# The down-projection of a hybrid trunk: sums that go on in PSUM across groups of products, with operands kept in place

## The chip, the core and the metric

One core of one Trainium2 chip runs a two-layer hybrid encoder trunk in one launch. Five engines work side by side: TensorE (PE, with its weight loads as PEld), VectorE (DVE), ScalarE (ACT), GpSimd (POOL) and SyncE (SP), which here issues nearly all DMAs. Each takes its own instructions in order and waits on semaphores of the others. The metric is the time of one execution on the device, in microseconds.

## The reference

Each of DEPTH = 2 layers mixes tokens with three kinds of heads and then runs a gated feed-forward part. What the change touches is the last line, with D_FF = 2816, 1024 tokens and a width of 1024, all in float32:

```
hf = rms_norm(x, ffn_norm[l]) @ w_up[l]
gate, val = hf[..., :D_FF], hf[..., D_FF:]
gate = depthwise_conv(gate, conv_w[l], conv_b[l])
x = x + (gelu(gate) * val) @ w_down[l]
```

## The kernel before

Features lie on the partitions, 128 at a time, so the residual `X` is eight tiles of 128 x 1024. A layer runs the projections and the heads, the output projection (`out_proj`), then `up` and `down`.

`up` walks over 22 blocks `f` of 128 hidden features. For each, 84 matmuls of 128x512 make seven products (L1114); DVE adds them into `v` and `g` (L1121), `gate` scales and convolves (POOL L1154, L1155 and L1159; DVE L1156 and L1157; ACT L1158), DVE multiplies (L1144), and SP stores the block `t` to a scratch array in DRAM, `hid` in the profile's names (L1145). The next block's weights come as `wraw`; their split forms `wo` lie in the ring of ten `w` slots.

`down` computes a 1024 x 2816 by 2816 x 1024 product as a 2 x 2 block product with seven instead of eight multiplications: `W[k]` and `W[k + 11]` are the two halves of the hidden features, `h0` and `h1` the halves of outputs or tokens. Every operand is split in two, a rounded value and its rest (`split`, `split2`: ACT copies, DVE subtracts), and a product of two operands is three matmuls: high by high, high by rest, rest by high. A product thus takes 11 steps `k`, four column blocks `c` and three terms: 132 matmuls, 924 for seven, all at L1306. They run in four **groups**: groups 0 to 2 make two products each (`acc[0]` in the two `pa` tiles of two banks each, `acc[1]` in the four `pt` and `pb` banks), group 3 makes one. A group's steps run in the order that `orders` gives; the last three steps of a group are issued together, column by column (`DOWN_TAIL`), and `evacuate` empties each bank once, at its group's end.

The operands of a step come from `prep(g, k)`: up to five DMA loads of 256 KB (`load`, L1188, on SP), DVE differences and sums (`tt`, L1174), then the splits. Group 0 makes `dp` and `dq` (weights in half 0, hidden rows in half 1) and `dr = dp - dq`; the `k`-th pair lies in a ring that `DOWN_RINGS` names: `r` (8 slots), `w` (10) or `u` (13). Group 1 loads over `dp`, uses it up, and leaves `ds` for each `k`; group 2 loads `dz` and `dt`, adds `dz` to `ds`, and loads one half of `ds` anew for group 3. `dz`, `dy` and all the splits (`bo`, `bw`) share the 16 `x` slots, and `dt` has three half slots. The seven products go in part to several blocks of the output: groups 0 and 1 are copied to `du` tiles by ACT (L1256), and `late_adds` combines these on DVE during group 2, three operations a step, and adds them to `X`; groups 2 and 3 are added to `X` straight out of PSUM. The eight tiles `X` are loaded from DRAM (`mid`) in group 1, from step `DOWN_X` on.

The order on each engine isn't that of the code: a scheduler of the framework places each instruction when it can run by its own model, with the slots of the rings as limits, and the engines then keep that order.

Of the kernel before, what the change touches and what calls it, by code (L numbers as in the profile page):

```python
# [13 lines left out]
ALU = mybir.AluOpType  # L14
AX = mybir.AxisListType.X

P = 128
# [54 lines left out]
DOWN_RINGS = "rwrwrwwwuuu"  # L72
DOWN_ORDER = [10, 9, 8, 0, 2, 4, 1, 3, 5, 6, 7]
DOWN_X = 5
# [19 lines left out]
class Trunk:  # L94
# [1069 lines left out]

    def down(self, l, H, spill, out):
# [4 lines left out]
        X, kept, S, U, V, E, F, adds = [], {}, {}, [], [], [], [], []  # L1170
        orders = [list(range(n)), DOWN_ORDER, DOWN_ORDER[::-1], DOWN_ORDER[::-1]]

        def tt(out, a, b, op=ALU.subtract):
            nc.vector.tensor_tensor(out, a, b, op=op)  # L1174

        def split(src):
            o = self.split_x(src, None, self.xslot)
            return o[:, 0], o[:, 1]
# [11 lines left out]
        def prep(g, k):  # L1190
            if g == 0:
                slot = {"r": self.rslot, "w": self.wslot, "u": self.slot}[DOWN_RINGS[k]]

                p, q = kept[k] = slot([P, 2, 512], name="dp"), slot([P, 2, 512], name="dq")
                b = self.half([P, 512], "dt")
                load(p[:, 0], W[k][:, h0])
                load(b, H[k][:, h0])
                load(q[:, 0], W[k][:, h1])
                load(q[:, 1], H[k][:, h1])
                load(p[:, 1], H[k + n][:, h1])  # L1200
                one = split(p[:, 0]), split(b)
                r = self.slot([P, 2, 512], name="dr")
                tt(r, p, q)
                return [one, split2(r)]
            if g == 1:
                p, q = kept.pop(k)

                y = self.xslot([P, 2, 512], name="dy")
                load(p[:, 1], H[k][:, h0])
                load(y[:, 0], W[k + n][:, h1])  # L1210
                load(y[:, 1], H[k + n][:, h1])
                s = S[k] = (self.slot if len(S) < 9 else self.wslot)([P, 2, 512], name="ds")
                tt(p[:, 1], q[:, 1], p[:, 1])
                tt(y[:, 0], y[:, 0], q[:, 0], ALU.add)
                one = split(y[:, 0]), split(p[:, 1])

                tt(s, p, y)
                return [one, split2(s)]
            s = S[k]
            if g == 2:  # L1220

                z, b = self.xslot([P, 2, 512], name="dz"), self.half([P, 512], "dt")
                load(z[:, 0], W[k + n][:, h0])
                load(z[:, 1], H[k + n][:, h0])
                load(b, H[k + n][:, h1])

                tt(s, z, s, ALU.add)
                one = split(s[:, 0]), split(b)
                load(s[:, 0], W[k + n][:, h1])
                return [one, split2(z)]  # L1230
            return [None, split2(s)]

        def late_adds():

            for c2 in range(2):
                u, v, e, f = U[c2], V[c2], E[c2], F[c2]
                yield f, u, f
                for j in range(2):
                    x = X[2 * c2 + j][:, h0]
                    yield x, x, u[:, j]  # L1240

                yield v, v, f
                yield f, f, e
                yield e, e, v
                for j in range(2):
                    x, y = X[2 * c2 + j], X[4 + 2 * c2 + j]
                    yield x[:, h1], x[:, h1], f[:, j]
                    yield y[:, h0], y[:, h0], v[:, j]
                    yield y[:, h1], y[:, h1], e[:, j]
# [23 lines left out]
        for i, (g, k) in enumerate(steps):  # L1273
# [3 lines left out]
            if g == 2:  # L1277
                if m == 0:
                    adds = late_adds()
# [201 lines left out]
```

## Time and profile before

| | before |
|---|---|
| median of 3 runs | 2920.05 us (2918.1 to 2930.07) |
| the profiled execution | 2923.2 us |
| its span | 2921.4 us, 40354 instructions |
| mean granted TensorE clock | 0.987 |
| PE at L1306, layer 1 | from 1226.97 to 1468.40 us |
| PE at L1306, layer 2 | from 2675.20 to the last matmuls, which start at 2916.90 |

The profile follows one execution. Its rows name engine, line, operation, `out<-in` and shapes; what stands in brackets behind a row of the timeline is how long the engine sat idle before it, and what it then had waited for. A table of windows gives the busy time of each engine in stretches of the span, with the count of instructions, the TensorE clock that was granted (PEclk, 1.00 is full), the mean busy share of the 16 DMA engines and what they moved. The lines of the two tables above that carry the argument are quoted where they are used.

### The profile page before, as it was taken

The numbers are of one execution on the slowest core, as the hardware profiler recorded it, in microseconds if no ns is written. First come the engines' busy times: TensorE is split into PE (matmuls) and PEld (weight loads), VectorE is DVE, ScalarE is ACT, GpSimd is POOL, SyncE is SP. The second block draws the span as 40 slices with busy tenths as digits, with TensorE's granted clock in tenths as the row PEclk, the third lists the DMA queues.
The fourth block names the chain that finished last, engine by engine and source line by source line (L and its number), as shares of the span: only waits on it lengthen the run. The fifth ranks groups of instructions, "written<-read, shape, count | busy, mean of one in ns | idle before, by whom it ended". The sixth has DMA issues, their size and how long they took to land.

```text
span 2921.4 us, 40354 instructions
## 1 busy us (share of the span) xinstructions
PE 2797.9 (96%) x14984; PEld 2345.9 (80%) x14984; DVE 2260.8 (77%) x3082; ACT 1359.5 (47%) x2371; POOL 1236.8 (42%) x811
## 2 busy tenths in 40 slices
PE   8999999999999999899899999999999999998998
PEld 7999986777777787687699999777777787776876
DVE  5849678897788888888648495888967888888874
ACT  5526467786422222243435264677854222223432
POOL 2516545532366666410115265454323666664100
PEclk9999999999999999999999999999999999999999
DMA  4213262101222222654313043421022122226432
GB/s 146 84 32 102 73 155 69 44 16 65 94 73 86 73 87 80 216 181 154 103 53 84 24 113 99 113 69 44 15 88 85 66 87 80 84 76 248 166 124 96
DMA packets 152900, 273.64 MB, mean 94 GB/s; under 512 B 16512, under 2 KB 74112, under 8 KB 152704
## 3 DMA queue, kind: packets, MB, share of 16 engines
q1 hardware_dynamic: 142912, 241.71, 25.6%
q0 software_dynamic: 9792, 29.36, 3.8%
q8 instruction: 118, 1.93, 0.3%
q14 instruction: 78, 0.64, 0.1%
HBM read 201.80 MB, written 69.21 MB: 93 GB/s over the span
## 4 chain that ended last, share of the span: by engine, by line
PE 27%; DVE 9%; POOL 6%; DMA 5%; issue 3%; ACT 3%; SPq 0%; ACTq 0%; DVEq 0%; POOLq 0%
PE pa L269 5%; PE pa L281 4%; POOL ws L1059 3%; DVE wo L1064 3%; PE pb L860 2%; PE pa L774 2%; DMA wraw<-w_u 2%; PE pt L1306 2%; PE pa L1306 2%; PE pb L1306 2%; DMA dz<-hid 2%; PE pt L845 2%; POOL t L1159 1%; ACT wo L1063 1%; PE pb L619 1%
## 5 line engine op out<-in xcount | busy, mean ns | idle before, releaser
L1114 PE MATMUL pt<-bo,wo 128*128 128x512 f32 x1584 | 388.6, 397 | 29.6 <-DVE pu L1121 24.1
L1114 PEld LDWEIGHTS pt<-bo,wo 128*128 128x128 f32 x1584 | 297.0, 190 | 111.6 <-issue 35.1
L1114 PE MATMUL pb<-bo,wo 128*128 128x512 f32 x1584 | 381.7, 389 | 0.6 <-ACT rbc L1037 0.6
L1114 PEld LDWEIGHTS pb<-bo,wo 128*128 128x128 f32 x1584 | 297.0, 188 | 62.8 <-ACT rbc L1037 1.1
L281 PE MATMUL pa<-wh,xh 128*128 128x256 f32 (+1 forms) x864 | 263.6, 305 | 7.6 <-ACT xh L233 7.6
L281 PE MATMUL pa<-wh,xl 128*128 128x256 f32 (+1 forms) x864 | 262.1, 305 | 5.5 <-DVE xl L234 5.5
L774 PE MATMUL pa<-qk,qk 96*128 96x512 f32 (+1 forms) x896 | 258.1, 415 | 9.3 <-DMA qk<-bq 3.9
L281 PE MATMUL pa<-wl,xh 128*128 128x256 f32 (+1 forms) x864 | 262.0, 303 | 1.4 <-DVE wl L336 1.4
L1306 PE MATMUL pa<-bo,bo 128*128 128x512 f32 x792 | 206.9, 407 | 26.0 <-ACT bo L1016 22.1
L1064 DVE TENSOR_TENSOR wo<-ws,wo 128x512 fp32r<-128x512 f32 x176 | 216.0, 1244 | 8.6 <-ACT wo L1063 4.5
L1063 ACT ACTIVATE wo<-ws 128x512 fp32r<-128x512 f32 x176 | 102.0, 624 | 253.6 <-POOL ws L1059 209.9
L1306 PEld LDWEIGHTS pa<-bo,bo 128*128 128x128 f32 x792 | 152.3, 196 | 69.8 <-ACT bo L1016 28.6
L855 DVE TENSOR_TENSOR ptl<-pt,pth 128x512 fp32r<-128x512 f32 x240 | 161.9, 683 | 45.4 <-ACT pth L849 44.2
L774 PEld LDWEIGHTS pa<-qk,qk 96*128 96x128 f32 (+1 forms) x896 | 157.4, 191 | 40.0 <-issue 8.1
L809 DVE CUSTOM_DVE_ANT_0 pb<-pa,toep 128x1024 f32<-128x1024 f32 x128 | 153.7, 1218 | 45.1 <-PE pa L774 41.0
L849 ACT ACTIVATE pth<-pt 128x512 fp32r<-128x512 f32 x256 | 148.9, 597 | 76.3 <-PE pt L845 72.2
L793 POOL TENSOR_SCALAR pa<-pa,z 128x1024 f32<-128x1024 f32 x96 | 110.1, 1147 | 153.1 <-PE pt L845 102.8
L281 PEld LDWEIGHTS pa<-wh,xh 128*128 128x128 f32 x864 | 166.4, 193 | 7.7 <-ACT xh L233 7.6
L281 PEld LDWEIGHTS pa<-wh,xl 128*128 128x128 f32 x864 | 165.2, 192 | 6.1 <-DVE xl L234 5.9
L281 PEld LDWEIGHTS pa<-wl,xh 128*128 128x128 f32 x864 | 166.3, 192 | 1.9 <-DVE wl L336 1.6
L1064 DVE TENSOR_TENSOR wo<-wraw,wo 128x512 fp32r<-128x512 f32 x132 | 149.7, 1137 | 18.3 <-ACT wo L1063 16.1
L812 ACT ACTIVATE pb<-pb,nmb 128x1024 f32<-128x1024 f32 x128 | 147.1, 1151 | 32.7 <-DVE nmb L809 27.0
(324 smaller groups left out, 6900.0 us busy)
## 6 DMA issues: line engine op xcount, KB each, us to landing
wraw<-w_u SPq DMA_DIRECT2D x88, 512.0 KB, 4.0
hid<-t SPq DMA_DIRECT2D x44, 512.0 KB, 2.9
bk<-st SPq DMA_DIRECT2D x256, 48.0 KB, 1.7
qk<-bk POOLq DMA_DIRECT2D x32, 384.0 KB, 6.2
dt<-hid SPq DMA_DIRECT2D x44, 256.0 KB, 3.9
dp<-hid SPq DMA_DIRECT2D x44, 256.0 KB, 5.4
X<-xT SPq DMA_DIRECT2D x16, 512.0 KB, 5.3
wraw<-w_o SPq DMA_DIRECT2D x16, 512.0 KB, 3.7
```

Of the source, the lines that this page charges most:

```text
L269: nc.tensor.matmul(ps[:, hf * 512 : hf * 512 + 512], w, x[:, hf * 512 : hf * 512 + 512], start=first, stop=last)
L281: self.nc.tensor.matmul(ps, x[:, ts], w[:, k % kp, :cols], start=first, stop=last)
L774: nc.tensor.matmul(ps[:, hs], q[:rows, o + t * P : o + (t + 1) * P], kk[w][:rows, hs], start=w == 0, stop=w == 1)
L793: nc.gpsimd.tensor_scalar(e, e, z, 1.0, op0=ALU.mult, op1=ALU.mult)
L809: nc.vector.tensor_tensor_reduce(e, ps, self.toep[:, o : o + T], scale=-slope, scalar=3.0e38, op0=ALU.add, op1=ALU.min, accum_out=nm)
L812: nc.scalar.activation(e, e, AF.Exp, bias=nm, scale=-1.0, accum_out=z[:, t, i : i + 1])
L849: nc.scalar.activation(hi[:, kk], ps, AF.Copy)
L855: nc.vector.tensor_tensor(lo[:, kk], ps, hi[:, kk], op=ALU.subtract)
L1063: nc.scalar.activation(o[:, 0], src, AF.Copy)
L1064: nc.vector.tensor_tensor(o[:, 1], src, o[:, 0], op=ALU.subtract)
L1114: nc.tensor.matmul(ps, st, mv, start=k + u + v == 0, stop=k == 3 and u == 1)
L1306: nc.tensor.matmul(acc[j][c], a[u][:, c * P : (c + 1) * P], b[v], start=q + u + v == 0, stop=q == n - 1 and u == 1)
```

## The change

The seven products are grouped anew, so that one that goes to several output blocks is summed in one bank with the others that go there:

- Group 0 makes its two products in `acc[0]` and `acc[1]`. At its end DVE adds `acc[0]` to half `h0` of `X[c]`, and `acc[1]` to half `h1` of `X[4 + c]`; PSUM keeps both.
- Group 1 sums on into the same eight banks. At its end DVE adds both to half `h1` of `X[c]`.
- Group 2 sums on in `acc[0]` and starts `acc[1]` anew; at the end `acc[0]` goes to both halves of `X[4 + c]` (one 1024-wide addition from a broadcast bank), `acc[1]` to half `h0` of `X[c]`.
- Group 3 starts `acc[1]` anew and adds it to half `h0` of `X[4 + c]`.

So `du`, ACT's copies into it and `late_adds` are gone. `dp` and `dq` stay in their slots, loaded and computed over in place, through all four groups: steps 0 to 4 in `w` slots, steps 5 to 10 in `u` slots. Half loads go to `da` (half slots) in groups 0 and 1; group 2 has a further pair `dw`, in two `x` slots and then in `u` slots. All operands are split 1024 wide (`split2`). `X` comes in 16 half loads, from step 4 of groups 0 and 1 by the code. The number of matmuls, 924 per layer, and of loads, 132 per layer beside `X`, is the same. Lines move: matmuls are at L1287 after, `tt` at L1177, `load` at L1187.

```
-DOWN_RINGS = "rwrwrwwwuuu"
-DOWN_ORDER = [10, 9, 8, 0, 2, 4, 1, 3, 5, 6, 7]
-DOWN_X = 5
+DOWN_RINGS = "wwwwwuuuuuu"
+DOWN_ORDERS = [list(range(11)), list(range(11)), [5, 6, 7, 8, 9, 10, 0, 1, 2, 3, 4], [0, 1, 2, 3, 4, 5, 6, 7, 8, 9, 10]]
+DOWN_X = 4
...
+        def prep(g, k, m):
             if g == 0:
-                slot = {"r": self.rslot, "w": self.wslot, "u": self.slot}[DOWN_RINGS[k]]
+                slot = {"w": self.wslot, "u": self.slot}[DOWN_RINGS[k]]
                 p, q = kept[k] = slot([P, 2, 512], name="dp"), slot([P, 2, 512], name="dq")
+                a = self.half([P, 512], "da")
                 load(p[:, 0], W[k][:, h0])
+                load(p[:, 1], H[k][:, h1])
+                load(q[:, 1], H[k][:, h0])
                 load(q[:, 0], W[k][:, h1])
+                load(a, W[k + n][:, h1])
+                tt(p[:, 1], p[:, 1], q[:, 1])
+                tt(q[:, 0], q[:, 0], a, ALU.add)
+                (a11, t1), (s1, b11) = split2(p), split2(q)
+                return [(a11, b11), (s1, t1)]
+            p, q = kept[k]
             if g == 1:
+                a = self.half([P, 512], "da")
+                load(q[:, 1], H[k + n][:, h1])
+                load(a, W[k + n][:, h0])
+                tt(p, q, p)
+                tt(q[:, 0], a, p[:, 0])
+                return [split2(p), split2(q)]
+            if g == 2:
+                w = (self.xslot if m < 2 else self.slot)([P, 2, 512], name="dw")
+                load(w[:, 0], W[k + n][:, h1])
+                load(w[:, 1], H[k][:, h0])
+                load(q[:, 0], W[k + n][:, h0])
+                load(q[:, 1], H[k + n][:, h0])
+                tt(w[:, 0], w[:, 0], p[:, 0])
+                tt(w[:, 1], p[:, 1], w[:, 1])
+                load(p[:, 0], W[k + n][:, h1])
+                ops = [split2(w), split2(q)]
                 tt(p[:, 1], q[:, 1], p[:, 1])
+                return ops
+            return [None, split2(p)]
...
         def evacuate(g, j, c, ps):
-            if g < 2:
-                ts = ((U, V), (E, F))[g][j]
...
-                nc.scalar.activation(ts[c // 2][:, c % 2], ps, AF.Copy)
-                return
             x, y = X[c], X[4 + c]
+            if (g, j) == (0, 0):
+                add(x[:, h0], ps)
+            elif (g, j) == (0, 1):
+                add(y[:, h1], ps)
+            elif g == 1:
+                add(x[:, h1], ps)
+            elif (g, j) == (2, 0):
+                yv = y.rearrange("p (a t) -> p a t", a=2)
+                add(yv, ps.unsqueeze(1).broadcast_to([P, 2, 512]))
...
+                first = g if j and g > 1 else 0
...
+                                start=g == first and q + u + v == 0,
+                                stop=q == n - 1 and u == 1,
+                                skip_group_check=g > first,
```

**The start of layer 2's down-projection.** On DVE, before, from the end of the last block of `up` (`g`, `v` at L1121) on; `dr` is `dp - dq` of six steps, `bw` the first split of such a difference:

```order
L1121 TENSOR_TENSOR g_23568<-pu_23567,pt_23641 128x512
L1121 TENSOR_TENSOR v_23569<-pu_23567,pb_23655 128x512
L1174 TENSOR_TENSOR dr_23692<-dp_23678,dq_23679 128x1024
L1174 TENSOR_TENSOR dr_23712<-dp_23698,dq_23699 128x1024
L1174 TENSOR_TENSOR dr_23732<-dp_23718,dq_23719 128x1024
L1174 TENSOR_TENSOR dr_23782<-dp_23768,dq_23769 128x1024
L1174 TENSOR_TENSOR dr_23826<-dp_23812,dq_23813 128x1024
L1174 TENSOR_TENSOR dr_23870<-dp_23856,dq_23857 128x1024
L1156 SCALAR_TENSOR_TENSOR t_23668<-g_23568,pp,t_23668 128x1023
L1174 TENSOR_TENSOR bw_23695<-dr_23692,bw_23694 128x1024
```

The same engine and place after; `dp` and `dq` with numbers 23569, 23587, 23605 and 23653 are those of steps 0, 1, 2 and 3:

```order
L1177 TENSOR_TENSOR dp_23605<-dp_23605,dq_23606 128x512
L1177 TENSOR_TENSOR dq_23606<-dq_23606,da_23607 128x512
L1121 TENSOR_TENSOR g_23459<-pu_23458,pt_23532 128x512
L1177 TENSOR_TENSOR bw_23616<-dp_23605,bw_23615 128x1024
L1177 TENSOR_TENSOR dp_23569<-dq_23570,dp_23569 128x1024
L1177 TENSOR_TENSOR bw_23620<-dq_23606,bw_23619 128x1024
L1121 TENSOR_TENSOR v_23460<-pu_23458,pb_23546 128x512
L1156 SCALAR_TENSOR_TENSOR t_23559<-g_23459,pp,t_23559 128x1023
L1157 SCALAR_TENSOR_TENSOR t_23559<-g_23459,pp,t_23559 128x1023
L1177 TENSOR_TENSOR dp_23653<-dp_23653,dq_23654 128x512
L1177 TENSOR_TENSOR dq_23654<-dq_23654,da_23655 128x512
L1177 TENSOR_TENSOR dp_23587<-dq_23588,dp_23587 128x1024
```

The six differences in a row are gone; three steps are prepared and split by the time of up's last `v`, and the fourth stands behind the two operations of `gate` on the last `t`. On SP the loads there, after, are those of steps 0 (23570) and 1 (23587, 23588), with those of `X` and one of step 3 (`da`):

```order
L1187 DMA dq_23570<-w_d 128x512
L1187 DMA dp_23587<-w_d 128x512
L1187 DMA dp_23587<-hid_138 128x512
L1187 DMA X_23797<-mid_136 128x512
L1187 DMA X_23798<-mid_136 128x512
L1187 DMA X_23797<-mid_136 128x512
L1187 DMA da_23655<-w_d 128x512
L1187 DMA dq_23588<-hid_138 128x512
L1187 DMA dq_23588<-w_d 128x512
L1187 DMA X_23843<-mid_136 128x512
L1187 DMA X_23844<-mid_136 128x512
L1187 DMA X_23798<-mid_136 128x512
```

Before, SP had the loads of seven steps there, and the first two whole tiles of `X` behind them. After, all 16 half loads of `X` stand among those of steps 0 to 3, ahead of step 4's.

**The first change of groups in layer 2.** Before, DVE worked through the copies `du` in the third group, beside that group's `ds`, `bo` and `bw`:

```order
L1174 TENSOR_TENSOR du_24686<-du_24686,du_24656 128x1024
L1174 TENSOR_TENSOR X_24542<-X_24542,du_24192 128x512
L1174 TENSOR_TENSOR X_24544<-X_24544,du_24192 128x512
L1174 TENSOR_TENSOR du_24701<-du_24177,du_24701 128x1024
L1174 TENSOR_TENSOR ds_24482<-dz_24710,ds_24482 128x1024
L1174 TENSOR_TENSOR du_24656<-du_24656,du_24192 128x1024
L1174 TENSOR_TENSOR X_24450<-X_24450,du_24686 128x512
L1174 TENSOR_TENSOR X_24452<-X_24452,du_24686 128x512
L1174 TENSOR_TENSOR du_24207<-du_24207,du_24701 128x1024
L1017 TENSOR_TENSOR bo_24716<-ds_24482,bo_24716 128x512
L1174 TENSOR_TENSOR X_24542<-X_24542,du_24656 128x512
L1174 TENSOR_TENSOR X_24544<-X_24544,du_24656 128x512
```

After, DVE reads the banks at each group's end. These are the rows around the end of group 0 (`pa`, `pt`, `pb` are the banks, the `dp` and `dq` rows around them belong to group 1):

```order
L1177 TENSOR_TENSOR dq_23738<-da_24198,dp_23737 128x512
L1177 TENSOR_TENSOR dp_23963<-dq_23964,dp_23963 128x1024
L1177 TENSOR_TENSOR X_23797<-X_23797,pa_23623 128x512
L1177 TENSOR_TENSOR X_23843<-X_23843,pa_23624 128x512
L1177 TENSOR_TENSOR X_23889<-X_23889,pt_23625 128x512
L1177 TENSOR_TENSOR X_23890<-X_23890,pt_23626 128x512
L1177 TENSOR_TENSOR X_23935<-X_23935,pb_23627 128x512
L1177 TENSOR_TENSOR X_23936<-X_23936,pb_23628 128x512
L1177 TENSOR_TENSOR dq_23780<-da_24235,dp_23779 128x512
L1177 TENSOR_TENSOR dq_23826<-da_24274,dp_23825 128x512
L1177 TENSOR_TENSOR dq_23872<-da_24313,dp_23871 128x512
L1177 TENSOR_TENSOR X_23798<-X_23798,pa_23623 128x512
```

The additions to `X` have moved from the third group to the ends of groups 0 and 1, between preparations; PE's first matmul of group 0's last round on `pa` and those of group 1 wait for them.

**The third group of layer 2.** On SP before, loads of group 2 (`dz`, `ds`, `dt`) stand in the order of the steps, each pair of `dz` in the `x` slot of an earlier operand:

```order
L1188 DMA ds_24394<-w_d 128x512
L1188 DMA dt_24937<-hid_138 128x512
L1188 DMA dz_24848<-w_d 128x512
L1188 DMA dz_24848<-hid_138 128x512
L1188 DMA ds_24352<-w_d 128x512
L1188 DMA dt_24981<-hid_138 128x512
L1188 DMA dz_24892<-w_d 128x512
L1188 DMA dz_24892<-hid_138 128x512
L1188 DMA ds_24310<-w_d 128x512
L1188 DMA dt_25025<-hid_138 128x512
```

After, the weights and hidden rows of `dq` come one step after the other into their own slots, and `dw` follows:

```order
L1187 DMA dq_23780<-w_d 128x512
L1187 DMA dq_23780<-hid_138 128x512
L1187 DMA dp_23825<-w_d 128x512
L1187 DMA dq_23826<-w_d 128x512
L1187 DMA dq_23826<-hid_138 128x512
L1187 DMA dq_23872<-w_d 128x512
L1187 DMA dq_23872<-hid_138 128x512
L1187 DMA dq_23918<-w_d 128x512
L1187 DMA dq_23918<-hid_138 128x512
L1187 DMA dq_23964<-w_d 128x512
L1187 DMA dw_24428<-w_d 128x512
L1187 DMA dw_24428<-hid_138 128x512
```

The `dz` loads are gone; those of `dq` wait for group 1's split of the same `dq`, and no longer for a slot of the `x` ring.

More of the change, by code (lines that the diff above doesn't have):

```diff
@@ L1169, in down @@
         h0, h1 = slice(0, 512), slice(512, 1024)
-        X, kept, S, U, V, E, F, adds = [], {}, {}, [], [], [], [], []
-        orders = [list(range(n)), DOWN_ORDER, DOWN_ORDER[::-1], DOWN_ORDER[::-1]]
+        X, kept = [], {}
         def tt(out, a, b, op=ALU.subtract):
             nc.vector.tensor_tensor(out, a, b, op=op)
-        def split(src):
-            o = self.split_x(src, None, self.xslot)
-            return o[:, 0], o[:, 1]
         def split2(src):
@@ L1198, in prep @@
                 load(q[:, 0], W[k][:, h1])
[L1199 to L1204, printed above, removed]
-            if g == 1:
[L1206 to L1212, printed above, removed]
-                tt(p[:, 1], q[:, 1], p[:, 1])
[L1214 to L1249, printed above, removed]
@@ L1266, in evacuate, with residual @@
             else:
-                tt(y[:, h0], y[:, h0], ps, ALU.add)
+                add(y[:, h0], ps)
                 if out is not None:
                     load(out[4 + c][:, h0], y[:, h0])
-        steps = [(g, k) for g in range(4) for k in orders[g]]
-        ready, late, adds = [], [], iter(())
-        for i, (g, k) in enumerate(steps):
-            m = i % n
+        def residual(g, m):
+            c = m - DOWN_X
+            if not 0 <= c < 4:
+                return
+            if g == 0:
+                X.extend(self.rslot([P, T], name="X") for _ in range(2))
+                load(X[2 * c][:, h0 if c < 2 else h1], spill[2 * c][:, h0 if c < 2 else h1])
+                load(X[2 * c + 1][:, h0 if c < 2 else h1], spill[2 * c + 1][:, h0 if c < 2 else h1])
+            else:
+                load(X[2 * c][:, h1 if c < 2 else h0], spill[2 * c][:, h1 if c < 2 else h0])
+                load(X[2 * c + 1][:, h1 if c < 2 else h0], spill[2 * c + 1][:, h1 if c < 2 else h0])
+        steps = [(g, k, m) for g in range(4) for m, k in enumerate(DOWN_ORDERS[g])]
+        ready, late, acc = [], [], [None, None]
+        for i, (g, k, m) in enumerate(steps):
             while len(ready) < min(len(steps), i + 1 + DOWN_AHEAD):
                 ready.append(prep(*steps[len(ready)]))
-            if g == 2:
-                if m == 0:
-                    adds = late_adds()
-                for _ in range(3):
-                    op = next(adds, None)
-                    if op:
-                        tt(*op, ALU.add)
-            if g == 1 and len(X) < KC and m >= DOWN_X:
-                for c in (len(X), len(X) + 1):
-                    x = self.rslot([P, T], name="X")
-                    load(x, spill[c])
-                    X.append(x)
-            if m == 0:
-                acc = [None, None]
-                if g < 3:
-                    ps = [self.bank2([P, T]) for _ in range(2)]
-                    acc[0] = [p[:, h] for p in ps for h in (h0, h1)]
+            if g < 2:
+                residual(g, m)
+            if m == 0 and g == 0:
+                acc[0] = [p[:, h] for p in [self.bank2([P, T]) for _ in range(2)] for h in (h0, h1)]
+            if m == 0 and g != 1:
                 acc[1] = [self.bank1([P, 512], tag=t) for t in ("pt", "pt", "pb", "pb")]
```

23 lines of the change are left out of this document (11 added, 12 removed).

## Prediction

> **What bounds the kernel now.** The page comes first: the busy shares and the chain that ended last.
>
> ```profile
> span 2921.4 us, 40354 instructions
> PE 2797.9 (96%) x14984; PEld 2345.9 (80%) x14984; DVE 2260.8 (77%) x3082; ACT 1359.5 (47%) x2371; POOL 1236.8 (42%) x811
> ...
> PE 27%; DVE 9%; POOL 6%; DMA 5%; issue 3%; ACT 3%; SPq 0%; ACTq 0%; DVEq 0%; POOLq 0%
> ```
>
> PE is busy nearly throughout, so time can only come from two places: fewer matmuls, or stretches where PE waits or runs below full clock. The change leaves the 924 matmuls of a down-projection as they are (7 products, 11 k, 4 column blocks, 3 terms). So I ask next what the matmuls of L1306 take beyond their own rate. The chain of waits gives that rate, and the table of windows, for L1306 alone, cuts each layer's down-projection into its start, its first two groups, its third and its fourth:
>
> ```profile
> 1435.92 2.72 PE pa L1306 x12
> ...
> core 0: us, PE busy (x) PEld busy (x), PEclk, DMA share, GB/s
> 1226.97:1249.00 22.03, 15.76 (x60) 12.09 (x60) 0.85 1.02 372
> 1249.00:1366.00 117.00, 117.00 (x517) 96.87 (x517) 1.00 0.47 157
> 1366.00:1432.00 66.00, 53.40 (x189) 38.39 (x187) 0.90 0.40 128
> 1432.00:1468.40 36.40, 36.40 (x160) 29.96 (x160) 1.00 0.27 102
> 2675.20:2697.00 21.80, 14.66 (x52) 11.12 (x52) 0.84 1.05 392
> 2697.00:2821.00 124.00, 124.00 (x549) 102.71 (x548) 1.00 0.45 151
> 2821.00:2885.00 64.00, 50.14 (x184) 36.54 (x184) 0.92 0.35 112
> 2885.00:2917.30 32.30, 32.30 (x144) 26.59 (x142) 1.00 0.21 82
> ```
>
> 12 matmuls in 2.72 us make 0.2267 us each. The start of layer 1 holds 60, worth 13.6 us, in 22.03: 8.4 us too many. Layer 2's holds 52 (11.8 us) in 21.80: 10.0. The third group has 189 (42.8 us) in 66.00 and 184 (41.7 us) in 64.00: 23.2 and 22.3 too many. In the other four rows count times rate is the length within 0.5 us. So **63.9 us** of the two down-projections is not matmul work: 18.4 at the starts, 45.5 in the third groups. The clock column says that part of it is a lower clock, which follows the waits.
>
> The timelines of PE and DVE show the start, layer 2's here, with the last product of up ahead of it:
>
> ```profile
> 2669.64 3.00 PE L1114 MATMUL pt<-bo,wo 128*128 128x512 f32 x12 [3.60 <-DVE pu L1121]
> ...
> 2687.00 2.08 PE L1306 MATMUL pt<-bw,bw 128*128 128x512 f32 x4 [5.92 <-DVE bw L1174]
> ...
> 2666.81 0.69 DVE L1017 TENSOR_TENSOR bo<-dp,bo 128x512 fp32r<-128x512 f32 x1 [4.09 <-ACT bo L1016]
> ...
> 2676.01 8.61 DVE L1174 TENSOR_TENSOR dr<-dp,dq 128x1024 f32<-128x1024 f32 x6
> 2684.54 1.27 DVE L1156 SCALAR_TENSOR_TENSOR t<-g,pp,t 128x1023 f32<-128x1023 f32 x1
> 2685.74 1.21 DVE L1174 TENSOR_TENSOR bw<-dr,bw 128x1024 fp32r<-128x1024 f32 x1
> ```
>
> DVE takes its work in order, and six subtractions, which need the loads of six steps, stand ahead of the first `bw` of a second product. PE waits 5.92 us for that `bw`. The 3.60 us above belong to up: its product waits for DVE, which waited 4.09 us at a first operation of down.
>
> The third group repeats one chain per step, here in the chain of waits of layer 1, with one step of PE and SP's total wait of layer 2's down:
>
> ```profile
> 1399.14 0.69 DVE bo L1017
> ...
> 1399.85 0.32 SPq L1188
> ...
> 1400.26 0.38 SPq L1188
> ...
> 1400.70 4.79 DMA dz<-hid
> ...
> 1405.58 1.24 DVE ds L1174
> ...
> 1406.90 0.64 ACT bo L1016
> ...
> 2837.71 4.96 PE L1306 MATMUL pa<-bo,bo 128*128 128x512 f32 x12 [2.20 <-ACT bo L1016]
> ...
> SPq L1188 <- DVE bo L1017: 80.1, 28, 8.8
> ```
>
> A `dz` load can start only when DVE has finished with an earlier step's buffer. Transfer, `ds`, `bo` and the next issue then run one after another: some 8 us a step, where PE needs 24 × 0.2267 = 5.44. Between waits of 1 to 3 us the clock drops as well: 12 matmuls took 4.96 us instead of 2.72.
>
> **The change, part by part.**
>
> *Third group: buffers in place.* The `dz` ring goes. After, the weights and hidden rows of group 2 are loaded into `dq`, which is free once group 1 has split it, and into `dw` buffers in slots that earlier steps gave up; the loads stand in SP's row many steps ahead. The chain above loses its transfer. What a step still needs is priced from the timelines of DVE and ACT and from the groups of lines:
>
> ```profile
> 2808.05 1.21 DVE L1174 TENSOR_TENSOR du<-du,du 128x1024 f32<-128x1024 f32 x1
> 2809.18 1.22 DVE L1174 TENSOR_TENSOR ds<-dz,ds 128x1024 f32<-128x1024 f32 x1
> ...
> 2811.46 1.28 DVE L1174 TENSOR_TENSOR X<-X,du 128x512 f32<-128x512 f32 x2
> 2812.66 1.22 DVE L1174 TENSOR_TENSOR du<-du,du 128x1024 f32<-128x1024 f32 x1
> ...
> 2913.47 0.69 DVE L1174 TENSOR_TENSOR X<-X,pt 128x512 f32<-128x512 f32 x1 [14.00 <-PE pt L1306]
> ...
> 2762.30 1.06 ACT L1183 ACTIVATE bw<-ds 128x1024 fp32r<-128x1024 f32 x1
> ...
> L1256 ACT ACTIVATE du<-pa 128x512 f32<-128x512 f32 x8 | 4.8, 594 | 6.5 <-PE pa L1306 6.5
> ```
>
> From start to start a 1024-wide DVE operation takes 1.13 us (2809.18 less 2808.05) and a 512-wide one 0.60 (half of 2812.66 less 2811.46). A step of group 2 has three of 0.60 and two of 1.13 after, 4.1 us, against two and two, 3.5, before; PE needs 5.44, ACT two splits, 2.1. PE stays the bound if supply is ahead. Five loads of 256 KB per 5.44 us are 241 GB/s, and the start rows above moved 372 and 392. Term: **−45.5 us**, bounds 0 (the chain comes back in another buffer) and −45.5.
>
> *Start and first change of groups.* After, each step's two preparations are followed by its own splits, and steps 0 to 2 are prepared among up's last operations; PE no longer waits for six steps' loads. But SP has put X's 16 half loads among those of steps 0 to 3. At 392 GB/s 256 KB take 0.67 us, X 10.7 us in all: step 3's loads are then complete some 36 × 0.67 = 24 us after the first went out at about 2660, at 2684, and PE asks for step 3 at 2675.2 + 3 × 5.44 = 2691.5. So loads have some 4 us to spare after 3 us of preparation. What is late next is **DVE itself**. Between up's last `v` and the first addition out of a bank stand 57 operations: 31 of 1.13, 24 of 0.60 and two of 1.2, 51.8 us. PE has 252 matmuls there, 57.1 us, from 2675.2 to 2732.3. DVE can't start on it at 2676.1 (2675.40 and 0.69, the row of `v`), since the first two need POOL's `t`. The timeline of DVE and that of POOL:
>
> ```profile
> 2675.40 0.69 DVE L1121 TENSOR_TENSOR v<-pu,pb 128x512 f32<-128x512 f32 x1 [0.86 <-PE pb L1114]
> ...
> 2668.33 2.37 POOL L1159 TENSOR_TENSOR t<-t,rbc 128x1024 f32<-128x1024 f32 x1 [8.24 <-ACT t L1158]
> ...
> 2677.12 4.16 POOL L1155 TENSOR_SCALAR t<-g,pp 128x1024 f32<-128x1024 f32 x1
> 2698.93 10.80 POOL L1159 TENSOR_TENSOR t<-t,rbc 128x1024 f32<-128x1024 f32 x1 [17.65 <-ACT t L1158]
> ```
>
> That `t` is there at 2681.3, so DVE ends at 2681.3 + 51.8 = 2733.1. A second wait follows, for the last `t` of L1159 before L1144: 2.37 us long it is covered by the five operations ahead, 10.80 us long (beside a dense DVE) it costs some 7. So PE is 1 to 8 us late at the first change, wherever it takes that time: at step 4, whose preparations stand behind L1144, or at the bank. I take 5 per layer, nearer to the 10.80 us, since DVE is dense here: −18.4 + 10 = **−8.4 us**, bounds −18.4 and 0. Up's own wait of 3.60 I leave, since DVE again has a down operation that waits for a load ahead of up's `v` and `pu`; bounds −7 and +7 for both layers, as it may vanish or double.
>
> Here the clock matters too. A PE idle of 2.20 us was followed by 12 matmuls at 0.41 us: the wait cost twice its length. The Trainium skill (TensorE: Matmul & The Clock Gate, Part 1: The HAM clock gate) says that the array falls to half clock after an idle window of about 3.4 us; read as one gap, the stalls that I leave would cost their length only. The row differs: shorter gaps, close together, were followed by half speed. The measurement decides.
>
> *Second and third change.* Removed are ACT's 16 copies of `du` (0.594 us each, hidden, since ACT is busy 47%) and DVE's 24 late additions, 8 of 1.13 and 16 of 0.60: 18.6 us a layer. Added are 16 additions out of banks in groups 0 and 1, and four of group 2's become 1024 wide: 16 × 0.60 + 4 × 0.53 = 11.7. One from PSUM (0.69) costs what one from SBUF does (1.28 for two). A bank that goes on summing may not be written while DVE reads it. At these two changes PE's row leaves each bank for 24 matmuls (5.4 us) or more before it returns there; at the first it is 6 (1.4 us). The eight additions of the second change take 4.8 us, with at most 2.9 of other work between two. DVE has 4.0 × 11 = 44 us of group 1's work in 60 of PE's and can be ahead. I take 1 us for each of these four changes, bounds 0 and 5 (a step's DVE work ahead of the addition): **+4 us**.
>
> *The rest.* X's half loads move the same bytes. The end after the last matmul is as before: four additions and stores.
>
> **Sum.** −45.5 − 8.4 + 4 = −49.9: the profiled execution, 2923.2 us, would be 2873.3. It stands 3.2 above the median of the runs, 2920.05; against that the forecast is **2870 us**. All bounds at their best, −63.9 − 7, give 2849.
>
> **Rivals.**
>
> (a) *The start stays.* X's loads keep the transfers saturated, and the in-order DVE waits for each step's last one. For it: the DMA share of 1.02 and 1.05 at both starts, X's loads put earlier. Against: 4 us to spare. Then −45.5 + 4 = −41.5: 2878; with a late first change on top, 2886.
>
> (b) *The third group is only half cured.* SP's queue is one, and a load whose slot isn't free stops those behind it, as the 80.1 us of waits show. If group 2 keeps half its loss: −22.8 − 8.4 + 4 = −27.2: 2893.
>
> (c) *The additions hold PE.* One mechanism, at the six group changes: PE restarts a bank only when DVE's addition out of it is through, and DVE takes that behind preparations. The price is the queued DVE work per change. The forecast has 14 us of it already; at 64 us, 10.7 a change, everything is given back, and at 13.5 (three steps' preparations) the sum is −63.9 + 81 = +17: 2937, slower. For it: DVE stands 4 us for one transfer in the third group, and the first change has no slack. Against: at the others it has. The Trainium skill (PSUM — Partial Sum Buffer, PSUM bank collisions raise a hardware error) has two engines kept apart on one bank, the rule behind this; no row of before shows a bank read amid its sum, since each was emptied once, at its end.
>
> (d) *Little comes of it.* Waits of 8 to 10.5 us a change: −63.9 + 48 to 63, so 2904 to 2919.
>
> **How the numbers follow.** The forecast has 0.56 (2849 to 2877), (a) 0.16 (to 2887), (b) 0.12 (to 2905), (d) 0.09, (c) 0.07. What a measurement of this kernel can tell from no change is about 0.5%, 14.6 us. So faster 0.84, same 0.09, slower 0.07. The range from 2850 to 2900 takes in the forecast, (a) and most of (b).
>
> **What would show it.** Right: third-group windows with PE busy throughout at clock 1.00, no `dz` in the chain, PE waits at the start below 4 us each, waits of PE on DVE `X` below 2 us at the second and third change, below 8 at the first. Wrong: such waits of 10 us or more (c), waits on `bw` behind DMA `dw` or `dq` in the third group (b), a wait of 5 us or more before the second step (a), or up's last product waiting more than 3.60 us.

## The result, and the profile after

The changed kernel takes 2880.97 us, the median of four runs (2879.85 to 2882.84), against 2921.89 for the kernel before in the same comparison (2918.1 to 2930.07): a ratio of 0.9857, with a 95% interval from 0.9834 to 0.9879. The forecast was 2870, with a range from 2850 to 2900. The profiled executions agree: the span falls by 43.4 us. The page of after, its first rows and its chain by engine and by line:

```profile
span 2878.0 us, 40091 instructions
PE 2782.9 (97%) x14984; PEld 2346.7 (82%) x14984; DVE 2253.6 (78%) x3044; ACT 1338.6 (47%) x2273; POOL 1214.2 (42%) x811
...
PE 56%; DVE 16%; POOL 11%; DMA 7%; issue 6%; ACT 5%; SPq 0%; ACTq 0%; POOLq 0%; DVEq 0%
PE pa L269 10%; PE pa L281 10%; POOL ws L1059 6%; DVE wo L1064 6%; PE pa L1287 6%; DMA wraw<-w_u 5%; PE pb L860 5%; PE pa L774 5%; PE pb L1287 4%; PE pt L1287 4%; PE pt L845 3%; POOL t L1159 3%; ACT wo L1063 2%; PE pt L619 1%; PE pb L619 1%
```

The busy times of PE, DVE, ACT and POOL have hardly moved. The chain's shares can't be set beside those of before: before they sum to 53%, since that chain was followed back only to about 1376 us, and after to the whole span. What has changed is its content: before, `dz` transfers of 3.5 to 4.8 us stood in it one after the other; after, no transfer stands in it within either down-projection. The table of windows for L1287 alone shows the down-projection of layer 2, cut at its start, the first change of groups, and the groups behind it (columns as before: length, PE, PEld, granted clock, DMA share, GB/s):

```profile
2654.77:2676.00 21.23, 21.23 (x94) 17.60 (x94) 1.00 1.05 389
2676.00:2712.00 36.00, 36.00 (x160) 29.43 (x158) 1.00 0.65 225
2712.00:2725.00 13.00, 5.87 (x16) 4.54 (x16) 0.74 0.53 166
2725.00:2788.00 63.00, 63.00 (x279) 52.16 (x279) 1.00 0.42 133
2788.00:2848.00 60.00, 60.00 (x267) 49.67 (x266) 1.00 0.37 131
2848.00:2874.00 26.00, 26.00 (x116) 21.31 (x114) 1.00 0.07 25
```

All but one row are full, at clock 1.00: the start, although the DMA engines stand at 1.05 there as before, and both rows that hold the third group. One row isn't: 13.00 us at the first change of groups hold 16 matmuls, worth 3.6 us, so 9.4 are lost; in layer 1 the same row has 12.50 us with 15 matmuls, so 9.1. The timeline of PE, from up's last products on (behind a row: the idle time ahead of it and what ended that):

```profile
2642.96 0.94 PE L1114 MATMUL pb<-bo,wo 128*128 128x512 f32 x3 [2.07 <-DVE v L1121]
2647.61 5.24 PE L1114 MATMUL pt<-bo,wo 128*128 128x512 f32 x12 [3.71 <-DVE pu L1121]
2652.69 2.24 PE L1114 MATMUL pb<-bo,wo 128*128 128x512 f32 x9
2654.77 2.88 PE L1287 MATMUL pa<-bw,bw 128*128 128x512 f32 x12
...
2719.28 5.25 PE L1287 MATMUL pa<-bw,bw 128*128 128x512 f32 x12 [7.13 <-DVE X L1177]
```

From 2654.77 to 2712 PE never stops. Then it waits 7.13 us until DVE has read the first bank. What follows are 12 matmuls in 5.25 us, at a granted clock of 0.53, where 12 elsewhere take 2.88: another 2.4. Up's last block waits at two places, 2.07 and 3.71, where before it waited at one, 3.60.

The 43.4 us thus come out as follows. A down-projection now takes 219.2 us from first matmul to last (1228.12 to 1447.34 in layer 1). Before, it was 241.4 and 242.1, so 45.1 us are gone in the two layers. The stretches ahead, up among them, have grown by 1.15 us in layer 1 and 0.63 in layer 2. 45.1 − 1.8 = 43.3.

Two questions are left for experiments. Why is PE held at the first change, and for so long? And was the third group cured for the reason that the prediction gave?

### The profile page after: what moved, and what is told of

Read it like the earlier page. It is cut to its first block, busy times and chain, and to the rows that moved or that the text cites. A ratio compares the mean times of both kernels' runs of the same rounds, so it can differ in the third digit from the quotient of the medians.

```text
span 2878.0 us, 40091 instructions
## 1 busy us (share of the span) xinstructions
PE 2782.9 (97%) x14984; PEld 2346.7 (82%) x14984; DVE 2253.6 (78%) x3044; ACT 1338.6 (47%) x2273; POOL 1214.2 (42%) x811
## 4 chain that ended last, share of the span: by engine, by line
PE 56%; DVE 16%; POOL 11%; DMA 7%; issue 6%; ACT 5%; SPq 0%; ACTq 0%; POOLq 0%; DVEq 0%
PE pa L269 10%; PE pa L281 10%; POOL ws L1059 6%; DVE wo L1064 6%; PE pa L1287 6%; DMA wraw<-w_u 5%; PE pb L860 5%; PE pa L774 5%; PE pb L1287 4%; PE pt L1287 4%; PE pt L845 3%; POOL t L1159 3%; ACT wo L1063 2%; PE pt L619 1%; PE pb L619 1%
## 5 line engine op out<-in xcount | busy, mean ns | idle before, releaser
L855 DVE TENSOR_TENSOR ptl<-pt,pth 128x512 fp32r<-128x512 f32 x240 | 162.0, 684 | 45.5 <-ACT pth L849 44.2
L1287 PE MATMUL pa<-bw,bw 128*128 128x512 f32 x616 | 178.3, 398 | 14.3 <-DVE X L1177 14.3
L1154 POOL TENSOR_TENSOR g<-g,rbc 128x1024 f32<-128x1024 f32 x44 | 108.5, 2466 | 115.8 <-DVE g L1121 115.8
```

The lines of the kernel that those rows point to most:

```text
L855: nc.vector.tensor_tensor(lo[:, kk], ps, hi[:, kk], op=ALU.subtract)
L1287: nc.tensor.matmul(acc[j][c], a[u][:, c * P : (c + 1) * P], b[v], start=g == first and q + u + v == 0, stop=q == n - 1 and u == 1, skip_gr ...
```

## The experiments

Twelve kernels ran, six edits of after (e1 to e4, e8 and e12) and six of before. `issue_after(i)` is the framework's way to put the instructions inside it behind instruction `i` in the order that is made. All ratios are against the kernel before on the same chip.

### First change of groups

DVE's timeline in after shows what it does ahead of the first bank:

```profile
2715.07 1.22 DVE L1177 TENSOR_TENSOR dp<-dq,dp 128x1024 f32<-128x1024 f32 x1
2716.21 1.28 DVE L1177 TENSOR_TENSOR dq<-da,dp 128x512 f32<-128x512 f32 x2
2717.41 1.21 DVE L1177 TENSOR_TENSOR dp<-dq,dp 128x1024 f32<-128x1024 f32 x1
2718.55 1.27 DVE L1177 TENSOR_TENSOR X<-X,pa 128x512 f32<-128x512 f32 x2
```

There is no idle time in these rows: the additions don't wait for PE. PE waits for them, and they stand behind preparations of group 1. Whether these are needed so early is what the next kernel tries.

**e1_behind**: the differences of group 1's last five steps and those of the first two `dw` go behind the last addition out of group 0's banks.

```
+                with self.tc.issue_after(fence[0].ins) if k > 5 else nullcontext():
+                    tt(p, q, p)
-                tt(p, q, p)
...
+                with self.tc.issue_after(fence[0].ins) if m < 2 else nullcontext():
+                    tt(w[:, 0], w[:, 0], p[:, 0])
+                    tt(w[:, 1], p[:, 1], w[:, 1])
...
         def add(x, ps):
+            fence[:] = [tt(x, x, ps, ALU.add)]
```

> Seven DVE operations of groups 1 and 2 that stood ahead of the additions at the first change (five 1024-wide differences of steps 6 to 10 and the two of the first dw, 6.9 us) are ordered behind them; nothing else changes. If the 7.1 us wait of PE there is DVE's backlog, it falls below 1.5 us, the 12 matmuls behind it run at full clock (2.7 us instead of 5), and each layer gains 7 to 9 us: 2863 to 2867 us. If reading the banks itself holds PE, the wait stays above 5 us, and if DVE is short of time in groups 0 and 1 together, the wait turns up at the second change: in both cases 2877 to 2884 us.

Measured: 2864.85 us (2860.53 to 2869.45), ratio 0.9803 [0.9784, 0.9822]. PE's row at the first change of layer 1:

```profile
1288.43 3.02 PE L1289 MATMUL pa<-bw,bw 128*128 128x512 f32 x12 [0.23 <-DVE X L1177]
```

7.14 us have become 0.23, in layer 2 nothing, and the 12 matmuls run at full speed again. The work of DVE is the same; only its order differs. So what holds PE is the queue ahead of the additions on DVE.

**e2_pairs**: at the end of groups 0 to 2, both columns of a `pa` tile are finished before either is read. (`DOWN_TAIL` is 2: the steps that a group issues together at its end, column by column, are two, not three as the part on the kernel before has it.)

```
-                    if m == n - 1 and ops[j] is not None:
-                        evacuate(g, j, c, acc[j][c])
+                    if m == n - 1 and ops[j] is not None and (j == 1 or c % 2):
+                        for e in (c,) if j else (c - 1, c):
+                            evacuate(g, j, e, acc[j][e])
```

> The columns of one pa tile are finished before either is read, so that PE does not wait for the addition out of a tile's first bank before it writes the second. If the backlog theory holds, PE has 12 more matmuls, 2.7 us, before it needs DVE's first addition: the wait of 7.1 us falls to 4 to 5 us and the time to 2874 to 2877 us. If the order of the columns does not matter (DVE's last addition decides), the time stays at 2879 to 2883 us.

Measured: 2877.96 us (2876.92 to 2881.59), ratio 0.9855 [0.984, 0.987], between the two ranges that were expected and not to be told from after. The totals of PE's waits around the first change (us, times, longest):

```profile
PE pa L1287 <- DVE X L1177: 5.0, 1, 5.0
```

The wait is 2.1 us shorter, by the matmuls that now run ahead of it. That PE returns to the tile early is thus the smaller part of the matter.

**e3_both** is both edits at once: e1's and e2's.

```
+                with self.tc.issue_after(fence[0].ins) if k > 5 else nullcontext():
...
+                    if m == n - 1 and ops[j] is not None and (j == 1 or c % 2):
```

> Both edits together. Backlog theory: no wait of PE above 0.5 us at the first change, and 9.4 us gained in each layer: 2860 to 2865 us. If groups 0 and 1 are bound by DVE altogether, the gain is below 5 us: 2876 to 2881 us.

Measured: 2859.82 us (2857.77 to 2860.43), ratio 0.979 [0.9775, 0.9804], the fastest kernel here. The table of windows has the two down-projections whole:

```profile
1227.59:1437.03 209.44, 209.44 (x924) 173.35 (x923) 1.00 0.53 179
2644.30:2853.80 209.50, 209.50 (x924) 173.32 (x923) 1.00 0.49 168
```

924 matmuls at 0.2267 us are 209.5: nothing is left to gain here but matmuls. On DVE it is now the additions that wait, for PE, and the five differences follow behind:

```profile
2701.63 1.28 DVE L1177 TENSOR_TENSOR X<-X,pa 128x512 f32<-128x512 f32 x2 [0.81 <-PE pa L1289]
...
2708.17 5.76 DVE L1177 TENSOR_TENSOR dp<-dq,dp 128x1024 f32<-128x1024 f32 x5
```

### Up's last block

What is left in e3 are up's own waits. **e8_up_first** keeps e3's edits, with eight differences in place of five behind the additions (`k > 2`; the expectation says nine), and puts the preparations of the down-projection's first steps behind up's second addition to `pu`.

```
-            add(u3, u2, p7)
+            self.fence = nc.vector.tensor_tensor(u3, u2, p7, op=ALU.add)
...
+                with self.tc.issue_after(self.fence.ins):
+                    tt(p[:, 1], p[:, 1], q[:, 1])
+                    tt(q[:, 0], q[:, 0], a, ALU.add)
+                    (a11, t1), (s1, b11) = split2(p), split2(q)
```

> Both edits of the third run, with nine instead of five 1024-wide differences behind the additions at the first change, and with DVE's first operations of down behind the last pu addition that up's fourth product needs. If down's operations in DVE's queue made up wait (1.8 and 3.7 us, and half clock behind them), these waits go and 5 to 8 us per layer are gained over the third run: 2844 to 2850 us. If DVE has no time to spare, PE waits at down's first steps or at a change of groups instead: 2855 to 2865 us.

Measured: 2866.94 us (2864.2 to 2874.49), ratio 0.9811 [0.9796, 0.9826]. Each of its runs is slower than each of e3's, and the median lies above both ranges that were expected. DVE now stands idle for 1.98 us until a load of `dq` is there, at 2646.70, and PE waits for `bw` in turn. **e12_up_mid**, with the same eight differences, takes an earlier operation, up's first addition to `pu`, and leaves step 0's differences ahead of it.

```
-            add(u2, u2, p6)
+            self.fence = nc.vector.tensor_tensor(u2, u2, p6, op=ALU.add)
...
+                with self.tc.issue_after(self.fence.ins) if k else nullcontext():
+                    tt(p[:, 1], p[:, 1], q[:, 1])
+                    tt(q[:, 0], q[:, 0], a, ALU.add)
+                with self.tc.issue_after(self.fence.ins):
+                    (a11, t1), (s1, b11) = split2(p), split2(q)
```

> The third run's edits with nine instead of five differences behind the additions; on DVE only the splits of step 0 and all of steps 1 and 2 stand behind up's first pu addition, so that DVE does not idle as in the eighth run. If up's last waits are paid by queue order alone, the wait on pu (3.7 us) and the half clock behind it go, 4 to 6 us per layer: 2848 to 2853 us. If groups 0 and up's end are bound by DVE's work, what is gained there comes back as waits on bw at down's first steps: 2858 to 2866 us.

Measured: 2862.44 us (2858.67 to 2863.86), ratio 0.9799 [0.9784, 0.9813], no gain over e3. The totals of PE's waits over up's end and the first group of layer 2, in e3:

```profile
PE pt L1114 <- DVE pu L1121: 3.7, 1, 3.7
PE pb L1114 <- DVE v L1121: 1.7, 1, 1.7
```

The same totals in e12:

```profile
PE pa L1291 <- DVE bw L1177: 1.9, 2, 1.1
PE pt L1114 <- DVE pu L1131: 1.6, 1, 1.6
PE pt L1291 <- DVE bw L1177: 1.4, 1, 1.4
PE pb L1291 <- DVE pu L1121: 0.6, 1, 0.6
```

5.4 us of waits for up's results have become 5.5 us, most of them for the down-projection's splits. In e3 DVE is busy for all of the 14.60 us from 2629.70 to the down-projection's start at 2644.30, so these two orders only chose who waits. That no order does better isn't shown. One operation there, the `bw` at 2631.81, takes 3.01 us where its kind takes 1.22, and it stands ahead of the `pu` that PE waits for; a later section comes back to such rows.

### Third group: why it was slow

**e4_dz_ring**, an edit of after, tests the prediction's reason. The second operand of group 2 is loaded into a fresh tile of the `x` ring again, as `dz` was, and no longer into `dq` in place.

```
                 w = (self.xslot if m < 2 else self.slot)([P, 2, 512], name="dw")
+                q = self.xslot([P, 2, 512], name="dz")
```

> The new grouping is kept, but group 2 loads its second operand into a new tile of the x ring (dz) instead of into dq. If it was the place of the operands that took the 22 us per layer out of the third group, waits of PE on bw behind DMA dz come back there, 10 to 25 us per layer: 2900 to 2930 us. If it was the removal of the late additions and copies, the third group stays free of waits: 2879 to 2884 us.

Measured: 2880.37 us (2876.78 to 2885.25), ratio 0.9862 [0.9846, 0.9879], the same as after. All of PE's waits from the first change of layer 2 to the end:

```profile
PE pa L1288 <- DVE X L1177: 7.0, 1, 7.0
```

The third group stays clean, so the place of this operand is not what cured it. DVE waits 8.5 us for `dz` transfers there (from 2785 to 2836), but PE doesn't wait for DVE.

**e6_no_late**, an edit of before, tests that the late additions were in the way. Groups 0 and 1 are left out of the result: neither copied nor added.

```
             if g < 2:
-                ts = ((U, V), (E, F))[g][j]
...
-                nc.scalar.activation(ts[c // 2][:, c % 2], ps, AF.Copy)
                 return
...
             if g == 2:
-                if m == 0:
-                    adds = late_adds()
...
+                pass
```

> The kernel before without the 16 copies to du and the 24 late additions of each layer; groups 0 and 1 are thus left out of the result. If these were what held the third group, its loss falls by over 15 us per layer: below 2895 us. By the queue theory only the waits while DVE was full with them go, 2 to 5 us per layer: 2911 to 2918 us.

Measured: 2917.58 us (2910.9 to 2921.85, ten runs), ratio 0.9983 [0.9971, 0.9994]. PE's waits in layer 1's third group, before:

```profile
PE pa L1306 <- ACT bo L1016: 10.3, 7, 2.9
```

And without the late additions:

```profile
PE pa L1297 <- ACT bo L1016: 11.5, 6, 2.6
```

So 18.6 us of DVE work per layer, taken away together with ACT's copies, is worth some 4 us in all. What is left to test is SP's order. In before a step of group 2 loads `dz` (two halves) and `dt`, and loads the first half of `ds` anew behind that step's split. **e5_dt_order** puts `dt` behind its own step's `dz`.

```
-                load(z[:, 1], H[k + n][:, h0])
-                load(b, H[k + n][:, h1])
+                own = load(z[:, 1], H[k + n][:, h0])
+                with self.tc.issue_after(own.ins):
+                    load(b, H[k + n][:, h1])
```

> The kernel before, with one order on SP changed: in group 2 a step's dt load stands behind the dz loads of the same step, and no longer ahead of those of two steps earlier. If the third group waited because dt, with three half slots, blocked the dz loads behind it in SP's queue (the queue theory), its loss of 22 to 23 us per layer falls below 8 and the time to 2876 to 2895 us. If the x ring or DVE's late additions set the pace there, the loss stays above 18 us per layer: 2912 to 2924 us.

Measured: 2920.4 us (2911.89 to 2927.04, ten runs), ratio 0.9997 [0.9985, 1.0008]. One step of the chain of waits in layer 1:

```profile
1394.48 0.70 DVE bo L1017
1395.20 0.33 SPq L1188
...
1395.63 0.38 SPq L1188
1396.06 4.32 DMA dz<-hid
1400.46 1.24 DVE ds L1174
1401.79 0.64 ACT bo L1016
1402.45 0.70 DVE bo L1017
```

The loop is as in before, 7.97 us from `bo` to `bo` (1402.45 less 1394.48), where PE needs 5.44. **e9_reload** leaves `dt` and moves the other load that waits for a split: `ds` is loaded anew three steps later.

```
+                if len(held) == 3:
+                    reload(own)
...
-                load(s[:, 0], W[k + n][:, h1])
+                held.append(k)
```

> The kernel before, with the reload of ds for group 3 issued three steps later on SP, behind the dz loads of that later step; dt stays where it was. If the reload, which can't go before DVE has split that step, was what closed the chain through SP's queue, the third group's loss of 22 us per layer falls below 10: 2880 to 2900 us. If dt, which also stands ahead of dz and waits for an earlier step's split, closes it just as well, the loss stays above 18: 2914 to 2924 us.

Measured: 2909.55 us (2907.25 to 2923.65, ten runs), ratio 0.9959 [0.9943, 0.9975], a gain of 12 to 15 us that is clear of noise and between the two ranges that were expected. **e10_reload_dt** does both.

```
+                own = load(z[:, 1], H[k + n][:, h0])
+                with self.tc.issue_after(own.ins):
+                    load(b, H[k + n][:, h1])
+                if len(held) == 3:
+                    reload(own)
...
-                load(s[:, 0], W[k + n][:, h1])
+                held.append(k)
```

> The reload three steps later and dt behind the dz of its own step. Queue theory in its second form (a reload or a dt ahead of dz on SP closes the loop of split, issue and transfer): the third group's loss falls below 8 us per layer, 2874 to 2892 us. If neither matters (the x ring or the transfers themselves set the pace), it stays above 18: 2914 to 2924 us.

Measured: 2881.94 us (2881.07 to 2883.58), ratio 0.9855 [0.9828, 0.9883]. The row of SP's waits for that split, in layer 2's down-projection, was 80.1 us before. The next three rows are counted from 2674 us on, as that one can be; e10's down-projection starts 19 us earlier, and with that stretch its 12.1 are 12.7. In e5:

```profile
SPq L1188 <- DVE bo L1017: 70.4, 18, 7.5
```

In e9:

```profile
SPq L1188 <- DVE bo L1017: 49.5, 21, 6.7
```

And in e10:

```profile
SPq L1188 <- DVE bo L1017: 12.1, 6, 4.2
```

PE's waits in layer 2's third group, in e9 and then in e10:

```profile
PE pa L1318 <- ACT bo L1016: 10.0, 5, 3.3
PE pa L1318 <- DVE bo L1017: 1.4, 1, 1.4
```

```profile
PE pa L1319 <- DVE bo L1017: 1.4, 1, 1.4
PE pt L1319 <- ACT bw L1183: 0.2, 1, 0.2
```

Only waits near the group's beginning are left. DVE, which waited 21.3 us for `dz` transfers in the third group of before (layer 2, from 2821 to 2885), waits for none of them in e10. Buffers, grouping and the work of every engine are those of before, and yet the kernel is as fast as after. Both loads that wait for a split must leave SP's head: `dt` alone gains nothing, the reload alone about a third of what both gain, since with one of them still there the next `dz` goes on waiting behind it.

### The start

**e7_interleave**, an edit of before, puts each `dr` behind the split of the step ahead, so that six differences no longer stand ahead of the first split.

```
                 r = self.slot([P, 2, 512], name="dr")
-                tt(r, p, q)
+                with self.tc.issue_after(fence[0].ins) if k else nullcontext():
+                    tt(r, p, q)
```

> The kernel before, with DVE's dr of a step of group 0 behind the split of the step before, instead of six dr in a row. If the six differences, which need six steps' loads, made the start late, the wait of 5.9 us falls below 2 and 6 to 9 us per layer are gained: 2903 to 2910 us. If the transfers, busy throughout, made it late, the wait stays at 4 us or more: 2916 to 2924 us.

Measured: 2924.84 us (2919.94 to 2932.41, ten runs), ratio 1.0009 [0.9999, 1.0018]. PE's waits from up's end to the end of the third group in layer 2:

```profile
PE pa L1309 <- ACT bo L1016: 11.3, 6, 2.6
PE pt L1114 <- DVE pu L1121: 4.4, 1, 4.4
PE pa L1309 <- DVE bo L1017: 3.1, 1, 3.1
PE pt L1309 <- DVE bw L1176: 1.4, 2, 0.9
PE pa L1309 <- ACT du L1259: 1.3, 1, 1.3
```

The wait for `bw`, 5.92 before, is 1.4 in two pieces. In return up waits 4.4 (3.60 before), the first change 1.3 and the third group's `bo` 3.1. The wait fell as the first reading expected, but the time stayed where the second had it: nothing is gained. **e11_before_orders** joins e7's edit with e10's:

```
+                with self.tc.issue_after(fence[0].ins) if k else nullcontext():
+                    tt(r, p, q)
...
+                if len(held) == 3:
+                    reload(own)
```

> The old grouping with both repairs of queue order: SP's as in the tenth run (reload three steps later, dt behind its dz) and DVE's as in the seventh (dr of a step behind the split of the step before). If the start and the third group are separate losses, the 6 us per layer that the seventh run took from the start show now, and the old grouping is faster than the new one as it was made: 2866 to 2874 us. If what is gained at the start is given back at the first change of groups, as in the seventh run, it stays at 2879 to 2886 us.

Measured: 2880.19 us (2877.49 to 2880.94), ratio 0.9858 [0.9842, 0.9875], the same as e10. The old grouping doesn't come near e3's 2859.82 by these orders.

## Why the prediction was right or wrong

**The third group: right in size, wrong in its cause.** The term was −45.5 us, and the windows of after have nothing left there. But the step said that a `dz` load could start only when DVE had finished with an earlier step's buffer, and that the chain goes because the `dz` ring goes. e4 brings such a buffer back for one operand and loses nothing. e10 keeps all the old buffers and loses only the group's first waits. What closed the loop was SP's single row: loads that wait for a split (`ds` anew, and `dt`) stood ahead of the next `dz`, which needs no split of that step, and that split needed a `dz` transferred. The prediction had this mechanism in hand, but in rival (b), as a way in which after might stay slow, not as what made before slow.

That either load alone keeps most of the loss is shown by e5 and e9; what exactly in after undoes the loop was not isolated. In its code no load waits for a split of group 2 itself: the one reload, of `dp`, waits only for the subtraction that makes `dw`, and the loads of `dq` wait for splits of group 1. SP does wait in after (57.9 us for `bw` splits in layer 2's down-projection), but it stays ahead, as the prediction said that it would: the last `dw` load of layer 2 goes out at 2801.02, DVE makes the group's last split at 2823.64, and from 2785 to 2836 DVE waits for no load. So the part of the step on the supply after holds; its part on what starved the group before doesn't, and that the term came out at its full size all the same is in part luck.

**Start and first change: direction right at the start, the remainder mis-sized.** The start's 18.4 us are gone altogether. The steps of the prediction hold: loads had time to spare, DVE itself was late next, and it showed at the bank. But the term left 5 us a layer there, and the windows show 9.1 and 9.4, so that the term is worth about zero and not −8.4. Two things were too small in it. First, DVE's end: counted from PE's start, the addition begins after 63.8 us (2718.55 less 2654.77), where the sum gave 57.9 (2733.1 less 2675.2). The count of 57 operations was right, and they begin 6.5 us after PE's start (2661.27), where the sum had 6.1. But they take 57.3 us and not 51.8. Of these 5.5 us, 2.2 are in one row, the second here, three times as long as its kind at 1.22. The first row, as long, stands ahead of the 57, in time that the sum had given to the wait for POOL's `t`. Another 2.4 are three waits for ACT's half of a split, of 0.66, 1.18 and 0.58, which the sum left out; the third row is the longest of them:

```profile
2655.68 3.42 DVE L1177 TENSOR_TENSOR dp<-dq,dp 128x1024 f32<-128x1024 f32 x1
...
2666.12 3.43 DVE L1177 TENSOR_TENSOR bw<-dp,bw 128x1024 fp32r<-128x1024 f32 x1
...
2683.86 1.22 DVE L1177 TENSOR_TENSOR bw<-dq,bw 128x1024 fp32r<-128x1024 f32 x1 [1.18 <-ACT bw L1182]
```

POOL's timeline has an operation at just the times of the two long rows:

```profile
2654.63 3.38 POOL L1154 TENSOR_TENSOR g<-g,rbc 128x1024 f32<-128x1024 f32 x1 [9.96 <-DVE g L1121]
...
2665.10 3.37 POOL L1159 TENSOR_TENSOR t<-t,rbc 128x1024 f32<-128x1024 f32 x1 [3.87 <-ACT t L1158]
```

The prediction feared that a dense DVE would stretch POOL (10.80 us); in these rows it is POOL that holds DVE. The Trainium skill (SBUF — State Buffer, Who interferes with whom) says that DVE and GpSimd share a pair of ports under an exclusive lock, and that a DVE instruction with two SBUF inputs contends with a GpSimd instruction that reads SBUF; the two pairs of rows agree. It goes the other way too: POOL's next operation, L1155 at 2658.12, took 3.12 us beside a `bw` of 1.21, where the same operation a block of up earlier, at 2633.41, with little of DVE's beside it, took 1.52. Second, a wait's price: the 7.13 us of idle were within the 8 that the prediction allowed, but the half clock behind them adds 2.4, though the prediction had quoted a row for just that.

**Second and third change: 0 in place of +4.** The 60 and 63 us around them are full at clock 1.00. DVE was ahead there, as argued; the unit of 1 us per change was a guess in the safe direction, and that it made up for half of the start's error is luck.

**Up's waits: left at no change, and +1.8 us measured** over all that stands ahead of the two down-projections. A second wait, for `v`, has come in, of 2.07 us. It lies within the bounds of ±7. One sign of being wrong that the prediction named did come, if barely: up's last product waits 3.71 us, where the limit was 3.60. e8 and e12 moved these waits and gained nothing.

Together: −45.5, then some +0.1 (2 × 9.3 in place of 18.4), 0 and +1.8, that is −43.6, where the span moved by 43.4. The forecast of 2870 lies 11 us below the median. 6.6 of these stand between the profiled executions (2873.3 forecast, 2879.85 measured), from the terms above; the rest is the step from the execution to the median, since before the profiled one stood 3.2 above its median and after 1.1 below. Of the rivals, (a) fell with the full start rows. (c) named the right mechanism, additions behind preparations, but at one change of three instead of all, and below its price. (b) and (d) didn't come, though (b)'s mechanism is the one that slowed before.

## What to carry to other kernels

A DMA queue that keeps its order is a resource with a head: look in its row for a load that waits for a compute step, and ask whether the load behind it feeds that same step; two loads moved in each step were worth as much here (0.9855) as the whole regrouping as it was made (0.9857). The two gains aren't the same one, though: the regrouping reached 0.979 once DVE's order was mended, and the old grouping, with its own DVE order changed, stayed at 0.9858. When a result is read out of PSUM while the sum goes on, put that read ahead of every preparation whose consumer is later: five 1024-wide differences and four half-wide ones behind the reads gave 0.9803 against 0.9857. A count of DVE operations by their usual duration is a lower bound, beside POOL and where splits wait for ACT, and a wait of PE can cost more than its length: 7.13 us of idle here were followed by 2.4 us lost to a lower clock.

## What was not expected of the hardware

How long PE stands is not enough to say what follows at lower clock. One gap of 3.60 us in before was followed by 12 matmuls in 3.00 us, at a granted clock of 1.00. The timeline of before has, in the other layer, 3.95 us with another outcome, at 0.61:

```profile
1219.79 4.58 PE L1114 MATMUL pt<-bo,wo 128*128 128x512 f32 x12 [3.95 <-DVE pu L1121]
```

In after, 12 matmuls took 5.25 us behind a gap of 7.13, and 5.24 behind one of 3.71 with another of 2.07 ahead of it, both at 0.53. A single gap of 1.57 us in e12 cost next to nothing (12 in 2.97). The Trainium skill (TensorE: Matmul & The Clock Gate, Part 1: The HAM clock gate) says that the clock is judged by a free-running activity window of about 3.4 us, so that the outcome varies with where a gap falls in it. That fits gaps near that length going either way; the half clock among waits of 1 to 3 us in the third group of before is no case of one idle window, and the runs don't settle it.
